# Stick attention: scores into the two x banks, logit sums on VectorE

## The chip, the cores and the metric

The kernel runs on one core of a Trainium2 chip. The metric is the device time of one execution in microseconds (us). Three timed executions of the kernel before gave 2578.15, 2578.38 and 2579.12 us, median 2578.38.

## The reference, cut to what matters

The program is two transformer blocks of two layers each, for 256 tokens of width 1024, in float32. The change lies in the mixer of the first layer of the first block, the stick-breaking attention with 16 heads of 64. For a query q and a key k before it (strictly causal):

```python
z = einsum(q, k) / 8
log_stay  = where(causal, log_sigmoid(-z), 0)
log_after = cumsum(log_stay, reverse=True) - log_stay
weights   = where(causal, exp(log_sigmoid(z) + log_after), 0)
out = weights @ v
```

log_sigmoid(-z) is -softplus(z), and softplus(z) = max(z, 0) + log(1 + exp(-|z|)). Taken together, the logarithm of a weight is z minus the sum of softplus over the keys from this one up to the query.

## The kernel before, in words

All stages run in one program; every engine executes its instructions in the order in which the Python code issues them (a manual schedule), and semaphores make one engine wait for another. `linear` (lines 364 to 366 are its matmuls) multiplies activations by weights that come from HBM, are split by ScalarE and VectorE into a high and a low part (lines 309 and 310) and are kept some tiles ahead. Its output blocks alternate between tiles of a pool of four PSUM banks (`self.ps()`, named p in the profile) and the two banks of `self.xp` (named xp), which are set aside for x in the last part of the program and lent to `linear` until then (`xp_lent`, lines 375 and 376). The odd blocks of a `linear` use xp, so the last block of the qkv product lies there until ScalarE has copied it out (line 775).

`stick` (from line 726) handles the 16 heads as eight pairs p. The scores are stored as keys by queries, 384 columns for each head of the pair. A pair goes through four stages:

- `stage_a(p)`: for each of the two heads e, four matmul instructions (lines 797 and 798) into a bank, then VectorE scales by 0.0625 (half of z) and adds the mask (line 799). Over both heads, 768 columns: VectorE forms min(-zh, zh) (line 800), ScalarE takes exp (line 801) and log(1+...) (line 803), and GpSimd forms zh - min (line 802).
- `stage_a2(p)`: GpSimd adds the two parts of softplus (line 808).
- `stage_b(p)`: TensorE sums softplus over keys with a triangular and an all-ones matrix (lines 817 to 819) into one bank for each head, VectorE forms 2·zh minus that (line 820), ScalarE takes exp (line 821).
- `stage_c(p)`: TensorE multiplies by v (lines 832 and 833) into one bank, and `put_split` writes the high part by ScalarE (line 543) and the low part by VectorE (line 544).

`round_(p)` (line 837) issues them as a pipeline: stage_a(p), stage_b(p-3), stage_a2(p), stage_c(p-5). Pairs 0 and 1 pass stage_a and stage_a2 earlier, beside the last block of the qkv product (deferred steps issued in `evac`). Rounds 2 to 7 thus have a new pair, rounds 3 to 10 a stage_b, rounds 5 to 12 a stage_c. Rounds up to 8 are issued before the output product `wo` begins, the last ones between its tiles. `wo` takes its first two banks from the same pool of four, after the bank that stage_c(2) used in round 7.

A round with all stages takes five banks of the pool of four: two in stage_a, two in stage_b, one in stage_c.

Of the kernel before, what the change touches and what calls it, by code (L numbers as in the profile page):

```python
# [9 lines left out]
AF = mybir.ActivationFunctionType  # L10
ALU = mybir.AluOpType
# [88 lines left out]
class Kernel:  # L100
# [625 lines left out]
    def stick(self):  # L726
        nc = self.nc
# [44 lines left out]
        def evac(n0, nw, ps):  # L772
            j, c = n0 // D, n0 % D
            for t in range(NT):
                nc.scalar.activation(qkv[j][t].ap[:, c:c + nw], ps[t], AF.Copy, scale=r()[:, t:t + 1])
            if c and j < 2:
                norm(j)
            if c and j == 1:
                self.defer(10, lambda: nc.scalar.preload_act_table_set("natural_log_exp_and_others"))
                self.defer(13, lambda: stage_a(0))  # L780
                self.defer(14, lambda: stage_a2(0))
                self.defer(15, lambda: stage_a(1))
                self.defer(16, lambda: stage_a2(1))

        mask = self.c[:, C_SBM:C_SBM + 384]
        tri, ones = self.c[:, C_TRI:C_TRI + 128], self.c[:, C_ONE:C_ONE + 128]
        st = {}

        def stage_a(p):


            q = qT[p // 4].ap[:, p % 4]
            zh, na, sp = (self.blk([128, 2, 384]) for _ in range(3))
            for e in range(2):
                k = kz[e][p // 4].ap[:, p % 4]
                z = self.ps()
                nc.tensor.matmul(z[:, :256], k[:, :128], q, start=True, stop=True)
                nc.tensor.matmul(z[:, 256:384], k[:, 128:], q[:, 128:], start=True, stop=True)
                nc.vector.scalar_tensor_tensor(zh.ap[:, e], z[:, :384], 0.0625, mask, op0=ALU.mult, op1=ALU.add)
            nc.vector.scalar_tensor_tensor(na.ap, zh.ap, -1.0, zh.ap, op0=ALU.mult, op1=ALU.min)  # L800
            nc.scalar.activation(sp.ap, na.ap, AF.Exp, scale=2.0)
            nc.gpsimd.tensor_tensor(na.ap, zh.ap, na.ap, ALU.subtract)
            nc.scalar.activation(sp.ap, sp.ap, AF.Ln, bias=1.0)
            st[p] = [zh, na, sp]

        def stage_a2(p):
            zh, m, sp = st[p]
            nc.gpsimd.tensor_tensor(sp.ap, m.ap, sp.ap, ALU.add)
            self.free(m)
            st[p] = [zh, sp]  # L810

        def stage_b(p):
            zh, sp = st[p]
            for e in range(2):
                inc = self.ps()
                s = sp.ap[:, e]
                nc.tensor.matmul(inc[:, :256], tri, s[:, :256], start=True, stop=False, skip_group_check=True)
                nc.tensor.matmul(inc[:, 128:256], ones, s[:, 256:], start=False, stop=True, skip_group_check=True)
                nc.tensor.matmul(inc[:, 256:384], tri, s[:, 256:], start=True, stop=True, skip_group_check=True)
                nc.vector.scalar_tensor_tensor(zh.ap[:, e], zh.ap[:, e], 2.0, inc[:, :384], op0=ALU.mult, op1=ALU.subtract)  # L820
            nc.scalar.activation(zh.ap, zh.ap, AF.Exp)
            self.free(sp)
            st[p] = zh

        def stage_c(p):
            w = st.pop(p)
# [10 lines left out]
        def round_(p):  # L837
            if 1 < p < 8:
                stage_a(p)
            if 0 <= p - 3 < 8:  # L840
                stage_b(p - 3)
            if 1 < p < 8:
                stage_a2(p)
            if 0 <= p - 5 < 8:
                stage_c(p - 5)
# [1258 lines left out]
```

## Time and profile before

| | |
|---|---|
| timed executions | 2578.15, 2578.38, 2579.12 us |
| profiled execution, its time | 2578.93 us |
| its span on the core | 2577.0 us |
| TensorE busy | 2332.2 us (91%) |
| VectorE busy | 1617.3 us (63%) |
| ScalarE busy | 897.1 us (35%) |
| GpSimd busy | 1058.4 us (41%) |
| mean granted TensorE clock | 0.97 of full speed |

The profiled execution took 2578.93 us, of which the span from the first to the last instruction is 2577.0 us. In the views, PE is TensorE's matmuls, PEld its weight loads, DVE VectorE, ACT ScalarE, POOL GpSimd, SP SyncE. L799 is line 799. A busy share over the whole span is a mean over stages with different limits; the stage that the change touches is a stretch of some 30 us around 280 us from the span's start.

### The profile page before, as it was taken

Reading aid. Unit: us, or ns where it says so; the run is one execution under the profiler, and the core shown is the slowest. Engines: PE = TensorE matmul, PEld = TensorE weight load, DVE = VectorE, ACT = ScalarE, POOL = GpSimd, SP = SyncE. Lnnn points to the kernel's source line nnn. Section 1 sums busy time; section 2 is a strip of 40 time slices with the busy share of each in tenths; the row PEclk is TensorE's granted clock in tenths of the full one; section 3 lists DMA queues with packets and bytes.
Section 4 is the critical chain, followed back from the end, with each engine's and each line's share of the span. In section 5 each row is a group of like instructions: output and inputs, shape, how many; then the busy total and the mean of one; then the engine's idle time right before and its main releaser. Section 6 shows DMA issues by size and latency. Waiting matters only on the chain.

```text
span 2577.0 us, 27968 instructions
## 1 busy us (share of the span) xinstructions
PE 2332.2 (91%) x8921; PEld 1516.9 (59%) x8921; DVE 1617.3 (63%) x3351; ACT 897.1 (35%) x1582; POOL 1058.4 (41%) x1119
## 2 busy tenths in 40 slices
PE   8999899999999999869998779997889898987877
PEld 7888688888888888755543234554344445432322
DVE  5555655555556556695687665854776764786744
ACT  5445554464445446521222211321222321222221
POOL 1002500000001001157677764655664665777775
PEclk9999999999999999989999989999999999999989
DMA  7555256565545654589999999999999999999998
GB/s 236 186 189 172 69 180 188 178 201 191 187 155 184 194 188 143 186 299 419 415 419 412 419 405 415 417 412 411 396 418 415 418 415 412 415 397 419 412 413 328
DMA packets 300786, 794.23 MB, mean 308 GB/s; under 512 B 26763, under 2 KB 66416, under 8 KB 300640
## 3 DMA queue, kind: packets, MB, share of 16 engines
q0 software_dynamic: 149152, 541.66, 52.1%
q1 hardware_dynamic: 151488, 250.78, 29.5%
q8 instruction: 72, 1.18, 0.2%
q14 instruction: 74, 0.61, 0.1%
HBM read 791.29 MB, written 1.05 MB: 307 GB/s over the span
## 4 chain that ended last, share of the span: by engine, by line
PE 61%; DMA 18%; DVE 12%; issue 4%; ACT 3%; POOL 1%; DVEq 0%; SPq 0%; POOLq 0%; ACTq 0%
PE p L1866 15%; DMA b<-in_peer_w_up,s 8%; PE p L364 6%; PE p L366 6%; PE p L365 6%; PE xp L364 6%; PE xp L366 6%; PE xp L365 6%; DMA b<-in_peer_w_down,s 6%; DVE b L1844 5%; PE p L1384 4%; DMA wr<-in_peer_w_q 3%; DMA wr<-in_dsa_w_in 1%; POOL b L1832 1%; PE p L1934 1%
## 5 line engine op out<-in xcount | busy, mean ns | idle before, releaser
L1866 PE MATMUL p<-b,s 128*128 128x512 f32 x2024 | 974.6, 621 | 147.1 <-ACT s L1864 93.9
L1866 PEld LDWEIGHTS p<-b,s 128*128 128x128 f32 x2024 | 380.6, 197 | 633.2 <-issue 490.9
L1844 DVE SCALAR_TENSOR_TENSOR b<-b,xp 128x1024 f32<-128x1024 f32 x512 | 610.2, 1212 | 141.9 <-DMA b<-in_peer_w_down,s 131.4
L1832 POOL DMA_INDIRECT b<-in_peer_w_down,s x512 | 482.8, 943 | 271.2 <-issue 95.4
L1832 POOL DMA_INDIRECT b<-in_peer_w_up,s x512 | 482.6, 942 | 259.4 <-issue 90.1
L310 DVE TENSOR_TENSOR wl<-wr,wh 128x1024 fp32r<-128x1024 f32 (+2 forms) x358 | 420.6, 1208 | 216.3 <-ACT wh L309 215.5
L309 ACT ACTIVATE wh<-wr 128x1024 fp32r<-128x1024 f32 (+2 forms) x358 | 361.6, 1040 | 199.6 <-PE xp L366 135.3
L653 POOL TENSOR_SCALAR s<-s 128x2 f32<-128x2 f32 (+1 forms) x12 | 4.8, 399 | 757.4 <-ACT b L662 727.3
L364 PE MATMUL p<-wh,b 128*128 128x512 f32 (+2 forms) x732 | 283.4, 387 | 1.5 <-DVE b L544 1.4
L366 PE MATMUL p<-wh,b 128*128 128x512 f32 (+2 forms) x732 | 277.1, 379 | 0.6 <-DVE b L544 0.3
L1864 ACT ACTIVATE s<-consts,s 128x128 f32<-128x128 f32 x506 | 175.3, 393 | 292.5 <-PE p L1866 169.8
L365 PE MATMUL p<-wl,b 128*128 128x512 f32 (+2 forms) x732 | 276.0, 377 | 0.1
L364 PE MATMUL xp<-wh,b 128*128 128x512 f32 (+3 forms) x716 | 273.1, 381 | 0.0
L366 PE MATMUL xp<-wh,b 128*128 128x512 f32 (+3 forms) x716 | 270.1, 377 | 0.0
L365 PE MATMUL xp<-wl,b 128*128 128x512 f32 (+3 forms) x716 | 269.9, 377 | 0.0
L366 PEld LDWEIGHTS p<-wh,b 128*128 128x128 f32 x732 | 137.9, 188 | 28.9 <-DVE b L548 2.9
L364 PEld LDWEIGHTS p<-wh,b 128*128 128x128 f32 x732 | 138.2, 189 | 27.0 <-DVE b L544 2.0
L1384 PE MATMUL p<-wr,b 128*128 128x512 f32 (+1 forms) x320 | 141.0, 566 | 13.9 <-DMA wr<-in_dsa_w_in 13.8
L365 PEld LDWEIGHTS p<-wl,b 128*128 128x128 f32 x732 | 138.4, 189 | 22.9 <-DVE wl L310 0.6
L366 PEld LDWEIGHTS xp<-wh,b 128*128 128x128 f32 x716 | 134.6, 188 | 24.6
L365 PEld LDWEIGHTS xp<-wl,b 128*128 128x128 f32 x716 | 134.8, 188 | 23.4
L364 PEld LDWEIGHTS xp<-wh,b 128*128 128x128 f32 x716 | 134.7, 188 | 23.5
(279 smaller groups left out, 1967.1 us busy)
## 6 DMA issues: line engine op xcount, KB each, us to landing
wr<-in_w_ffn_gu SPq DMA_DIRECT2D x176, 512.0 KB, 4.5
wr<-in_w_ffn_down SPq DMA_DIRECT2D x88, 512.0 KB, 4.5
wr<-in_dsa_w_in SPq DMA_DIRECT2D x56, 512.0 KB, 14.0
wr<-in_peer_w_q SPq DMA_DIRECT2D x40, 512.0 KB, 17.2
wr<-in_w_qkv SPq DMA_DIRECT2D x24, 512.0 KB, 4.5
wr<-in_w_ple_gate SPq DMA_DIRECT2D x16, 512.0 KB, 4.4
b<-in_peer_w_down,s POOLq DMA_INDIRECT x512, 9.1
b<-in_peer_w_up,s POOLq DMA_INDIRECT x512, 9.2
```

Of the source, the lines that this page charges most:

```text
L309: nc.scalar.activation(h, r, AF.Copy)
L310: nc.vector.tensor_tensor(l, r, h.bitcast(F32), ALU.subtract)
L364: nc.tensor.matmul(p[:, :nw], ah, h[:, kk, :], start=(k == 0), stop=False)
L365: nc.tensor.matmul(p[:, :nw], ah, l[:, kk, :], start=False, stop=False)
L366: nc.tensor.matmul(p[:, :nw], al, h[:, kk, :], start=False, stop=(k == last))
L653: nc.gpsimd.tensor_scalar(m, ss, mul, eps, op0=ALU.mult, op1=ALU.add)
L1384: nc.tensor.matmul(p[:, :nw], lhs(k0 + kk), w[:, kk, :], start=(k0 + kk == 0), stop=(k0 + kk == last), skip_group_check=True)
L1832: nc.gpsimd.indirect_dma_start(out=b.ap, out_offset=None, in_=(wd, wu)[s], in_offset=bass.IndirectOffsetOnAxis(ap=eidx[u][:, k:k + 1], axi ...
L1844: nc.vector.scalar_tensor_tensor(b.ap, b.ap, 1.0, self.xp, op0=ALU.mult, op1=ALU.mult, accum_out=acs[u][:, k:k + 1])
L1864: nc.scalar.activation(dg, self.ident, AF.Copy, scale=col)
L1866: nc.tensor.matmul(yp[n], dg, b.ap[:, n * 512:(n + 1) * 512], start=(h == 0 and k == 0), stop=(h == PH - 1 and k == (TOPK - 2 if u == nu - ...
L1934: nc.tensor.matmul(p[:, c * 128:(c + 1) * 128], w[:, kk, c * 128:(c + 1) * 128], xT1.ap[:, k], start=(k == 0 and c == 0), stop=(k == KD - ...
```

## The change

Pairs 2 to 7 write their scores into the two banks of xp, one for each head, instead of two banks of the pool; pairs 0 and 1 still use the pool. VectorE now scales by 0.125, so that the tile holds z itself. The instruction of line 800 writes min(-z, z) into the tile that exp and log then overwrite in place, so a pair holds two blocks of SBUF where it held three. GpSimd's two sums (lines 802 and 808) are gone; in stage_a2 one VectorE instruction forms max(z, 0) + log(1 + exp(-|z|)). In stage_b the subtraction needs no factor 2 and is a `tensor_tensor`. The order of the stages in `round_` is as it was.

```diff
         def stage_a(p):
             q = qT[p // 4].ap[:, p % 4]
-            zh, na, sp = (self.blk([128, 2, 384]) for _ in range(3))
+            z, sp = (self.blk([128, 2, 384]) for _ in range(2))
             for e in range(2):
                 k = kz[e][p // 4].ap[:, p % 4]
-                z = self.ps()
-                nc.tensor.matmul(z[:, :256], k[:, :128], q, start=True, stop=True)
-                nc.tensor.matmul(z[:, 256:384], k[:, 128:], q[:, 128:], start=True, stop=True)
-                nc.vector.scalar_tensor_tensor(zh.ap[:, e], z[:, :384], 0.0625, mask, op0=ALU.mult, op1=ALU.add)
-            nc.vector.scalar_tensor_tensor(na.ap, zh.ap, -1.0, zh.ap, op0=ALU.mult, op1=ALU.min)
-            nc.scalar.activation(sp.ap, na.ap, AF.Exp, scale=2.0)
-            nc.gpsimd.tensor_tensor(na.ap, zh.ap, na.ap, ALU.subtract)
+                s = self.xp[:, e * 512:(e + 1) * 512] if p > 1 else self.ps()
+                nc.tensor.matmul(s[:, :256], k[:, :128], q, start=True, stop=True)
+                nc.tensor.matmul(s[:, 256:384], k[:, 128:], q[:, 128:], start=True, stop=True)
+                nc.vector.scalar_tensor_tensor(z.ap[:, e], s[:, :384], 0.125, mask, op0=ALU.mult, op1=ALU.add)
+            nc.vector.scalar_tensor_tensor(sp.ap, z.ap, -1.0, z.ap, op0=ALU.mult, op1=ALU.min)
+            nc.scalar.activation(sp.ap, sp.ap, AF.Exp)
             nc.scalar.activation(sp.ap, sp.ap, AF.Ln, bias=1.0)
-            st[p] = [zh, na, sp]
+            st[p] = [z, sp]
 
         def stage_a2(p):
-            zh, m, sp = st[p]
-            nc.gpsimd.tensor_tensor(sp.ap, m.ap, sp.ap, ALU.add)
-            self.free(m)
-            st[p] = [zh, sp]
+            z, sp = st[p]
+            nc.vector.scalar_tensor_tensor(sp.ap, z.ap, 0.0, sp.ap, op0=ALU.max, op1=ALU.add)
 
         def stage_b(p):
...
-                nc.vector.scalar_tensor_tensor(zh.ap[:, e], zh.ap[:, e], 2.0, inc[:, :384], op0=ALU.mult, op1=ALU.subtract)
-            nc.scalar.activation(zh.ap, zh.ap, AF.Exp)
+                nc.vector.tensor_tensor(z.ap[:, e], z.ap[:, e], inc[:, :384], ALU.subtract)
+            nc.scalar.activation(z.ap, z.ap, AF.Exp)
```

## Rows read from the trace of the kernel before

**Rows 1.** Busy time by stretch: PE, PEld, DVE, ACT, POOL, then PEclk, DMA share, GB/s.

```profile
280.00:308.00 28.00, 20.31 (x126) 16.33 (x127) 22.06 (x31) 14.71 (x21) 25.70 (x13) 1.00 0.00 1
322.00:400.00 78.00, 78.00 (x365) 64.55 (x361) 44.48 (x50) 41.82 (x53) 0.90 (x2) 1.00 0.56 176
```

**Rows 2.** Timeline of VectorE: start, length, then [idle before <- who ended it].

```profile
276.10 0.96 DVE L800 SCALAR_TENSOR_TENSOR b<-b 128x768 f32<-128x768 f32 x1
276.98 1.02 DVE L799 SCALAR_TENSOR_TENSOR b<-p,consts 128x384 f32<-128x384 f32 x2
278.03 2.62 DVE L800 SCALAR_TENSOR_TENSOR b<-b 128x768 f32<-128x768 f32 x1
...
283.07 1.00 DVE L820 SCALAR_TENSOR_TENSOR b<-b,p 128x384 f32<-128x384 f32 x2
288.39 1.01 DVE L799 SCALAR_TENSOR_TENSOR b<-p,consts 128x384 f32<-128x384 f32 x2
...
294.78 0.42 DVE L544 TENSOR_TENSOR b<-p,b 128x256 fp32r<-128x256 f32 x1 [1.92 <-ACT b L543]
295.13 1.01 DVE L799 SCALAR_TENSOR_TENSOR b<-p,consts 128x384 f32<-128x384 f32 x2
...
307.08 0.42 DVE L544 TENSOR_TENSOR b<-p,b 128x256 fp32r<-128x256 f32 x1 [1.92 <-ACT b L543]
```

**Rows 3.** Timeline of GpSimd, and busy time of L800 alone in the rounds.

```profile
278.02 1.82 POOL L802 TENSOR_TENSOR b<-b,b 128x768 f32<-128x768 f32 x1 [3.96 <-ACT b L801]
...
276.90:304.40 27.50, 13.13 (x7) 1.00 0.05 17
```

**Rows 4.** Timeline of ScalarE.

```profile
277.10 0.84 ACT L801 ACTIVATE b<-b 128x768 f32<-128x768 f32 x1 [3.49 <-DVE b L800]
277.97 0.84 ACT L803 ACTIVATE b<-b 128x768 f32<-128x768 f32 x1
278.84 1.26 ACT L775 ACTIVATE b<-xp,s 128x512 f32<-128x512 f32 x2
...
279.43 0.68 ACT L775 ACTIVATE b<-xp,s 128x512 f32<-128x512 f32 x1
...
292.91 0.84 ACT L803 ACTIVATE b<-b 128x768 f32<-128x768 f32 x1
293.66 0.83 ACT L821 ACTIVATE b<-b 128x768 f32<-128x768 f32 x1
294.39 0.36 ACT L543 ACTIVATE b<-p 128x256 fp32r<-128x256 f32 x1
```

**Rows 5.** Timeline of TensorE: end of the qkv product, two pairs' scores, start of wo.

```profile
272.35 0.39 PE L366 MATMUL xp<-wh,b 128*128 128x512 f32 x1
...
281.27 0.67 PE L797 MATMUL p<-b,b 128*128 128x256 f32 x2 [1.64 <-DVE b L799]
...
282.43 0.38 PE L798 MATMUL p<-b,b 128*128 128x128 f32 x2
...
307.56 0.50 PE L364 MATMUL p<-wh,b 128*128 128x512 f32 x1 [0.85 <-DVE b L544]
```

**Rows 6.** A later idle stretch: TensorE's timeline, and busy time with PEclk.

```profile
1138.57 1.97 PE L589 MATMUL q<-consts,b 128*128 128x128 f32 x8 [5.79 <-DVE b L1159]
1140.33 3.68 PE L504 MATMUL p<-b,b 128*128 128x256 f32 x8
1144.42 1.89 PE L504 MATMUL p<-b,b 128*128 128x256 f32 x8
...
1137.00:1138.00 1.00, 0.00 (x0) 0.00 (x0) 0.85 (x6) 0.00 (x0) 0.54 (x1) 0.66 1.03 417
1144.00:1145.00 1.00, 1.00 (x8) 0.95 (x7) 1.00 (x3) 0.00 (x0) 0.69 (x2) 0.92 0.86 332
...
1110.00:1120.00 10.00, 8.13 (x23) 5.84 (x24) 8.88 (x29) 2.04 (x6) 2.81 (x3) 0.50 0.87 313
```

More of the change, by code (lines that the diff above doesn't have):

```diff
@@ L792, in stage_a @@
             q = qT[p // 4].ap[:, p % 4]
-            zh, na, sp = (self.blk([128, 2, 384]) for _ in range(3))
+            z, sp = (self.blk([128, 2, 384]) for _ in range(2))
             for e in range(2):
                 k = kz[e][p // 4].ap[:, p % 4]
-                z = self.ps()
-                nc.tensor.matmul(z[:, :256], k[:, :128], q, start=True, stop=True)
-                nc.tensor.matmul(z[:, 256:384], k[:, 128:], q[:, 128:], start=True, stop=True)
-                nc.vector.scalar_tensor_tensor(zh.ap[:, e], z[:, :384], 0.0625, mask, op0=ALU.mult, op1=ALU.add)
-            nc.vector.scalar_tensor_tensor(na.ap, zh.ap, -1.0, zh.ap, op0=ALU.mult, op1=ALU.min)
-            nc.scalar.activation(sp.ap, na.ap, AF.Exp, scale=2.0)
-            nc.gpsimd.tensor_tensor(na.ap, zh.ap, na.ap, ALU.subtract)
+                s = self.xp[:, e * 512:(e + 1) * 512] if p > 1 else self.ps()
[4 more added lines that the diff above has]
+            nc.scalar.activation(sp.ap, sp.ap, AF.Exp)
             nc.scalar.activation(sp.ap, sp.ap, AF.Ln, bias=1.0)
-            st[p] = [zh, na, sp]
+            st[p] = [z, sp]
         def stage_a2(p):
-            zh, m, sp = st[p]
-            nc.gpsimd.tensor_tensor(sp.ap, m.ap, sp.ap, ALU.add)
-            self.free(m)
-            st[p] = [zh, sp]
+            z, sp = st[p]
+            nc.vector.scalar_tensor_tensor(sp.ap, z.ap, 0.0, sp.ap, op0=ALU.max, op1=ALU.add)
         def stage_b(p):
-            zh, sp = st[p]
+            z, sp = st[p]
             for e in range(2):
@@ L819, in stage_b @@
                 nc.tensor.matmul(inc[:, 256:384], tri, s[:, 256:], start=True, stop=True, skip_group_check=True)
-                nc.vector.scalar_tensor_tensor(zh.ap[:, e], zh.ap[:, e], 2.0, inc[:, :384], op0=ALU.mult, op1=ALU.subtract)
-            nc.scalar.activation(zh.ap, zh.ap, AF.Exp)
+                nc.vector.tensor_tensor(z.ap[:, e], z.ap[:, e], inc[:, :384], ALU.subtract)
+            nc.scalar.activation(z.ap, z.ap, AF.Exp)
             self.free(sp)
-            st[p] = zh
+            st[p] = z
         def stage_c(p):
```

## The prediction

> **What bounds the kernel now.** I first read the busy time by stretch, to see what limits the place that is touched. In 280 to 308 us, where the rounds of the stick attention run, no engine is full: VectorE is busy for 22.06 of 28 us, GpSimd for 25.70, TensorE for 20.31, DMA does nothing; from 322 us on TensorE is busy for 78.00 of 78 us [rows 1]. So what the rounds lose or gain reaches the end undiminished: behind them stands an engine that is always busy, and the weights for it have long arrived. One bound for all of this: the stretch is about 30 of 2577 us, and 0.2% of the time, about what a measurement of this kernel can tell from no change, is 5.2 us.
>
> Then I read the timelines of VectorE, ScalarE, GpSimd and TensorE there. VectorE sets the pace in the order of the code: the two score instructions L799, then L800, then stage_b's two L820, then L544, and the next L799. Two things lengthen it. L800 takes 0.96 us alone, but 2.62 us at 278.03, where GpSimd's L802 began 0.01 us earlier and ran 1.82 us [rows 2, 3]; over the rounds it is busy 13.13 us, of which 0.16 us belong to the end of pair 1's [rows 3]. And where a round has a stage_c, VectorE stands idle for 1.92 us before L544, which needs ScalarE's L801, L803, L821 and L543 one behind the other [rows 2, 4]. The three rounds without stage_c take from 276.98 to 288.39, 11.41 us in all; the three with it run from there to the L544 at 307.08, whose end lets `wo` begin at 307.56 [rows 2, 5].
>
> **The change, part by part.**
>
> *GpSimd's sums go.* Nothing then lengthens L800: six times 0.96 instead of 13.13 - 0.16 = 12.97 us, 7.2 us less busy time [rows 2, 3]. The Trainium skill has this in "SBUF — State Buffer", section "Who interferes with whom": a VectorE instruction with two SBUF inputs and a GpSimd one that reads SBUF exclude each other, and the later one waits until the other has finished. By that rule alone the sum would be a gain; it is the fourth case below. GpSimd's queue holds only the loads of p for the next ffn behind the sums; they start earlier and stay hidden.
>
> *One VectorE sum comes, behind a wait.* It has the shape and operands of L800, so 0.96 us, and the next instruction starts 0.88 us after it (276.10 to 276.98 [rows 2]). Its tile comes from the log, L803, so VectorE's whole queue stands behind ScalarE in every round. From L799 on: L800 1.05 later (276.98 to 278.03 [rows 2]); L801 1.00 after that (276.10 to 277.10 [rows 2, 4]); L803 0.87 later (277.10 to 277.97); its end passed on another 0.87 later, as to the next on ScalarE at 278.84 [rows 4]. The new sum so starts at 1.05 + 1.00 + 0.87 + 0.87 = 3.79 and the next L799 at 4.67. The two subtractions of stage_b (1.00 us for both, from PSUM, like L820; dropping the factor 2 saves nothing, since L544, also a `tensor_tensor` from PSUM, takes 0.42 us for 256 columns and L820 pays about 0.5 for 384 [rows 2]) lie between L800 and the sum, in 1.93 to 2.93, inside the wait. Only their cover is new; uncovered they would cost 1.0 a round.
>
> *Rounds with a stage_c.* ScalarE goes on from L803 to L821 in 0.75 and L543 in 0.73 (292.91, 293.66, 294.39 [rows 4]), L544 follows in 0.39 and the next L799 in 0.35 (294.78, 295.13 [rows 2]). L544 starts at 1.05 + 1.00 + 0.87 + 0.75 + 0.73 + 0.39 = 4.79, behind the end of the sum (4.67), and the round takes 5.14. The sum costs nothing here: ScalarE's chain covers it.
>
> *The banks.* Three pool banks a round instead of five: TensorE need not wait for the pool and can run a round ahead, so VectorE never waits for it at full clock. I cost that at nothing beyond what the round lengths hold. `wo` still takes the bank that stage_c(2) leaves, so it still starts behind that L544.
>
> *Pair 2 waits for x's banks.* Before, pair 2's scores were done during the end of the qkv product, so its L799 came at 276.98 [rows 2]. Now they go into the banks that hold qkv's last block until L775 has copied them out. The first copy starts at 278.84 and takes 0.68, to 279.52 [rows 4]; TensorE starts 0.06 later as at 307.50 to 307.56 [rows 2, 5], at 279.58. A pair's scores take from 281.27 to 282.81, 1.54 us [rows 5], to 281.12; half of L799's 1.02 and two hand-overs of 0.03 follow, and L800 of pair 2 starts at 281.72. That corresponds to an L799 of both heads at 280.67, 3.7 us later than before. Pair 1's new sum waits for the log that ends at 278.81 [rows 4], is out of the way at 279.7, and is hidden by this; pair 0's lies in idle time of VectorE.
>
> *The clock.* TensorE ends the qkv product at 272.74 [rows 5] and now has nothing until 279.58: 6.8 us. After an idle stretch of 5.79 us the granted clock was 0.66 in the last stretch shown before work came, so it had gone to 1.2 GHz, and it was 0.92 at 1144 to 1145, 5.5 us after TensorE had begun to work back to back at 1138.57 [rows 6]. I take the same here. Eight matmuls of 256 columns took 3.68 us at half clock and 1.89 mostly at full, 0.224 more each [rows 6]; a pair's scores are six such lengths (four of 256, four of 128 columns), so pair 2 starts 1.34 us later still. Bounds: nothing, if the clock holds, and the third case below, if it stays low. The pairs behind cost nothing more: TensorE has scores 2, scores 3 and sums 0 queued (6 + 6 + 8 lengths at 0.46, 9.2 us without a pause), and VectorE needs those later than that. The Trainium skill speaks against the change here: "TensorE: Matmul & The Clock Gate", section "Why this matters for your kernels", asks for no idle gaps between bursts of matmuls, since they bring the half rate. Without that rule and that row the sum would be 1.34 smaller.
>
> **The sum.** Start 280.67 + 1.34 = 282.01. Rounds 2 to 4: 3 × 4.67 = 14.01 (11.41 before). Rounds 5 and 6: 2 × 5.14 = 10.28. Round 7 to L544: 4.79, and 0.48 to `wo` (307.08 to 307.56 [rows 2, 5]): 5.27. Together 29.56: `wo` starts at 311.57 instead of 307.56, **4.0 us later**. Everything behind has the same order and lengths. The profiled execution took 2578.93 us, 0.55 above the median of the runs and within their spread; 2578.93 + 4.0 would be its own time after, and against the median it is 2578.4 + 4.0 = **2582.4 us**. The six rounds between start and `wo` gain 30.58 - 29.56 = 1.0 us; the late start (3.7) and the clock (1.34) take 5.0.
>
> **The rivals.**
> 1. *The forecast*: x's banks come free late, the clock falls and returns. 0.60.
> 2. *The clock holds.* Only the idle stretch speaks for it falling; where in it the fall comes can differ. 2578.4 + 2.7 = 2581.1 us. 0.10.
> 3. *The clock stays low* (slower than before by more than can be missed). In 1110 to 1120 us it stayed at 0.50 for ten us with TensorE busy 81% [rows 6], so pauses can keep it down. A round's scores and sums are 14 lengths, 6.4 us at 0.46, and stage_c's up to 2.8 us more; take 7.8, against a round of 5.14: TensorE becomes the bound, 2.7 us a round. It decides once the low clock lasts into round 5, some 296 us. One round gives 2585.1, three 2590.5. Against it: the 9.2 us without a pause, longer than the 5.5 us that brought the clock back. 0.15.
> 4. *The freed port decides alone*: the wait for the log and the banks cost nothing, and VectorE's balance is 7.2 us less in L800 and 6 × 0.88 = 5.3 us more in the new sum: 2576.5 us. Against it: the order in the code puts the sum ahead of the next scores. 0.08.
> 5. *VectorE runs without any wait* from 276.98: scores and L800 1.05 + 0.88, new sum 0.88, stage_b's two 0.93, L544 0.35 (0.48 to `wo`), so rounds of 2.81, 3.74, 3.74, 4.09, 4.09 and 4.22, 22.7 us, `wo` 7.9 us earlier: 2570.5 us. This is the floor, and needs ScalarE's chain to be hidden, which the 1.92 us of rows 2 deny. 0.04.
>
> 0.03 is left for what none of these names, on both sides.
>
> **How the numbers follow.** 0.2% lies at 2573.2 and 2583.5 us. Slower: case 3 (0.15) and the upper sixth of case 1, since hand-overs of 0.03 to 0.06 a step over six rounds can add the 1.1 us that are missing (0.10): 0.25. Faster: case 5 and half of the rest, 0.05. Same: 0.70. The range 2577.5 to 2586.0 takes cases 1 and 2 with their bounds and the shorter half of case 3; case 5, most of case 4 and the longer half of case 3 stay outside.
>
> **What would show it.** VectorE's first L799 of pair 2 at about 281 and L800 of pair 2 at 283 (281.7 if the clock holds); granted clock 0.5 between about 278 and 285; all L800 at 0.96; VectorE idle some 0.8 us before each new sum, which ScalarE's log ends; rounds of 4.7 and then 5.1 us; `wo` at 311.6. Wrong would be the step on the banks if pair 2's scores start before L775 ends, the step on the sum if VectorE does not wait for the log, and the clock's if rounds 5 to 7 are longer than 5.3 us with TensorE as the one waited for.

## The result, and the profile after

The changed kernel takes 2593.92 us (median of five runs, 2591.47 to 2595.66); the kernel before takes 2578.96 us beside it (2578.15 to 2579.47). The ratio is 1.0058, with a 95% interval of 1.0046 to 1.0069: slower by 15 us, where 4 were forecast and the range ended at 2586.0. The direction had been given a chance of 0.25.

Two of the first lines of the profile's page, of the changed kernel:

```profile
span 2592.1 us, 27928 instructions
PE 2341.9 (90%) x8921; PEld 1524.6 (59%) x8921; DVE 1620.2 (63%) x3359; ACT 897.9 (35%) x1582; POOL 1028.0 (40%) x1103
```

Over the span hardly anything moves: GpSimd loses 30 us of busy time (1058.4 before), VectorE gains 3, TensorE 10. Such lines can't say where 15 us went. The span grew by 2592.1 - 2577.0 = 15.1 us, so the next thing to read is the stretch that was touched, by its two ends in TensorE's timeline: the last matmul of the qkv product and the first of `wo`. In the changed kernel:

```profile
273.19 0.40 PE L366 MATMUL xp<-wh,b 128*128 128x512 f32 x1
280.72 1.22 PE L796 MATMUL xp<-b,b 128*128 128x256 f32 x2 [7.13 <-ACT b L775]
283.09 1.22 PE L796 MATMUL xp<-b,b 128*128 128x256 f32 x2 [0.72 <-DVE b L798]
285.38 1.22 PE L796 MATMUL xp<-b,b 128*128 128x256 f32 x2 [0.65 <-DVE b L798]
...
302.46 1.22 PE L796 MATMUL xp<-b,b 128*128 128x256 f32 x2 [2.44 <-DVE b L798]
...
315.76 0.88 PE L796 MATMUL xp<-b,b 128*128 128x256 f32 x2 [1.91 <-DVE b L798]
...
323.60 0.50 PE L364 MATMUL p<-wh,b 128*128 128x512 f32 x1
```

From 273.19 to 323.60 are 50.41 us; before, 272.35 to 307.56 [rows 5], 35.21 us. The difference of 15.20 us is the whole loss. This distance is the yardstick of all that follows, and it is called **the stretch** from here on.

The rows also show how it was lost. The first pair that uses x's banks (pair 2) starts behind L775, as forecast. But then its second head's scores (283.09) wait for VectorE's L798, and that is the read of the *first* head's scores, in the other bank: the VectorE timeline of the same kernel has it at 282.47, ending at 283.03.

```profile
279.40 0.96 DVE L806 SCALAR_TENSOR_TENSOR b<-b,b 128x768 f32<-128x768 f32 x1 [1.78 <-ACT b L801]
282.47 0.56 DVE L798 SCALAR_TENSOR_TENSOR b<-xp,consts 128x384 f32<-128x384 f32 x1 [2.11 <-PE xp L797]
284.77 0.56 DVE L798 SCALAR_TENSOR_TENSOR b<-xp,consts 128x384 f32<-128x384 f32 x1 [1.74 <-PE xp L797]
285.36 0.96 DVE L799 SCALAR_TENSOR_TENSOR b<-b 128x768 f32<-128x768 f32 x1
288.11 0.96 DVE L806 SCALAR_TENSOR_TENSOR b<-b,b 128x768 f32<-128x768 f32 x1 [1.78 <-ACT b L801]
288.98 0.55 DVE L798 SCALAR_TENSOR_TENSOR b<-xp,consts 128x384 f32<-128x384 f32 x1
...
296.02 0.55 DVE L798 SCALAR_TENSOR_TENSOR b<-xp,consts 128x384 f32<-128x384 f32 x1
297.65 0.56 DVE L798 SCALAR_TENSOR_TENSOR b<-xp,consts 128x384 f32<-128x384 f32 x1 [1.07 <-PE xp L797]
...
301.86 0.55 DVE L798 SCALAR_TENSOR_TENSOR b<-xp,consts 128x384 f32<-128x384 f32 x1
...
308.92 0.55 DVE L798 SCALAR_TENSOR_TENSOR b<-xp,consts 128x384 f32<-128x384 f32 x1
...
315.16 0.55 DVE L798 SCALAR_TENSOR_TENSOR b<-xp,consts 128x384 f32<-128x384 f32 x1
```

(The lines have moved: L796 and L797 are the scores that were L797 and L798, L798 is the scaling that was L799, L799 the minimum that was L800, L806 the new sum.) Before, the two scalings were one row, x2, 1.02 us long [rows 2]. Now TensorE and VectorE take turns: scores of head 0, read, scores of head 1, read. At 285.38 the next pair's scores wait in the same way for the read of head 1, though their bank was read two us before (282.47 to 283.03). The view of who waited for whom, from 270 to 326 us, has these rows among others:

```profile
DVE b L798 <- PE xp L797: 10.8, 7, 2.1
...
PE xp L796 <- DVE b L798: 10.2, 7, 2.6
...
PE xp L796 <- ACT b L775: 7.1, 1, 7.1
...
DVE b L806 <- ACT b L801: 7.1, 5, 1.8
```

Columns are us in total, times, longest. Of the last row, one wait of 1.8 us belongs to pair 0's sum, ahead of the stretch. Waits of the last two kinds were in the forecast; the first two, each the other's cause, were not. And TensorE's clock, by stretch (after the busy times: granted clock, DMA share, GB/s):

```profile
278.00:295.00 17.00, 10.36 (x30) 8.31 (x31) 6.85 (x10) 5.98 (x8) 0.00 (x0) 0.52 0.05 18
302.00:306.00 4.00, 3.54 (x12) 3.13 (x13) 2.08 (x4) 0.27 (x1) 0.00 (x0) 0.57 0.00 0
316.00:320.00 4.00, 4.00 (x16) 3.44 (x15) 2.07 (x3) 1.28 (x2) 0.00 (x0) 0.57 0.00 0
```

It fell in the gap, as forecast, but stayed at 1.2 GHz for 17 us instead of 7, and fell twice more. Rounds 2 to 4, from one head-0 L798 to the next, took 6.51, 7.04 and 5.84 us (288.98 - 282.47, 296.02 - 288.98, 301.86 - 296.02), where 4.67 was forecast; rounds 5 and 6 took 7.06 and 6.24 us (308.92 - 301.86, 315.16 - 308.92), where 5.14 was.

### The profile page after: what moved, and what is told of

Read it like the earlier page. It is cut to its first block, busy times and chain, and to the rows that moved or that the text cites. A ratio compares the mean times of both kernels' runs of the same rounds, so it can differ in the third digit from the quotient of the medians.

```text
span 2592.1 us, 27928 instructions
## 1 busy us (share of the span) xinstructions
PE 2341.9 (90%) x8921; PEld 1524.6 (59%) x8921; DVE 1620.2 (63%) x3359; ACT 897.9 (35%) x1582; POOL 1028.0 (40%) x1103
## 4 chain that ended last, share of the span: by engine, by line
PE 61%; DMA 18%; DVE 11%; issue 5%; ACT 3%; POOL 2%; SPq 0%; DVEq 0%; POOLq 0%; ACTq 0%
PE p L1862 14%; DMA b<-in_peer_w_up,s 7%; DMA b<-in_peer_w_down,s 7%; PE p L364 6%; PE p L366 6%; PE xp L364 6%; PE xp L366 6%; PE xp L365 6%; PE p L365 6%; DVE b L1840 4%; PE p L1380 4%; DMA wr<-in_peer_w_q 2%; POOL b L1828 2%; DMA wr<-in_dsa_w_in 1%; PE p L504 1%
## 5 line engine op out<-in xcount | busy, mean ns | idle before, releaser
L310 DVE TENSOR_TENSOR wl<-wr,wh 128x1024 fp32r<-128x1024 f32 (+2 forms) x358 | 420.5, 1208 | 213.6 <-ACT wh L309 212.7
```

Of the source, the lines that this page charges most:

```text
L310: nc.vector.tensor_tensor(l, r, h.bitcast(F32), ALU.subtract)
```

## The experiments

Theory T: x's two banks are one tile (one buffer that the program allocates as a whole) for the program's synchronization, so a write into either waits for the last read of either. Rivals: C, the low clock after the gap is the main cost; W, the wait of VectorE's new sum for the log is; L, the late start of pair 2 is.

The experiments ran on two other chips, on which the part of the program from about 1000 us on takes longer: the kernel before takes 2721.54 and 2725.84 us there (medians), and nearly all runs of one kernel lie within 18 to 27 us. That spread is larger than most of the differences asked for, so the stretch, from one profile of each kernel, is the measurement to go by; ratios are given beside it. Up to `wo` the chips agree: the last matmul of the qkv product starts at 271.9 to 273.2 us in every run, and pair 1's first scaling 2.42 to 2.44 us behind it in all seven kernels with VectorE's sums, 2.70 or 2.71 in the three with GpSimd's. No kernel was profiled twice, so a few hundredths in the table mean nothing.

| kernel | stretch, us | against before |
|---|---|---|
| before | 35.21 | |
| changed | 50.41 | +15.20 |
| scores first | 40.13 | +4.92 |
| own tiles | 36.68 | +1.47 |
| banks only | 46.15 | +10.94 |
| sums only | 36.65 | +1.44 |
| pair 2 in the pool | 45.57 | +10.36 |
| clock held | 46.29 | +11.08 |
| reordered | 27.74 | -7.47 |
| order on before | 32.49 | -2.72 |

**Scores first.** One loop becomes two: the same instructions on each engine, in the same order there; only the reads now stand behind both writes in the program.

```diff
             for e in range(2):
...
                 nc.tensor.matmul(s[:, 256:384], k[:, 128:], q[:, 128:], start=True, stop=True)
-                nc.vector.scalar_tensor_tensor(z.ap[:, e], s[:, :384], 0.125, mask, ...)
+                sc.append(s)
+            for e in range(2):
+                nc.vector.scalar_tensor_tensor(z.ap[:, e], sc[e][:, :384], 0.125, mask, ...)
```

> The changed kernel, but the scores of both heads are issued before VectorE reads either. Theory T (the two banks are ordered as one tile: a write into either waits for the last read of either, so head 1's scores wait for head 0's L798 and TensorE can't run ahead): the waits of TensorE on L798 between the two heads (0.7 to 1.1 us in six pairs) and the VectorE waits on L797 that follow (1.1 to 1.7 us) go, rounds come down to 4.7 and 5.1 us, wo starts some 11 us earlier than at 323.6, about 2583 us. Theory C (the low clock after the gap is what costs, the order hardly matters): the clock still falls in the same gap, about 2590 us or more. Theory W (VectorE's wait for the log costs more than the 0.8 us a round seen): no change, 2593.

Measured: 40.13 us, 10.28 less than the changed kernel; ratio to before 1.0017 (0.9995 to 1.0039). TensorE and VectorE timelines of this run:

```profile
280.16 1.22 PE L797 MATMUL xp<-b,b 128*128 128x256 f32 x2 [7.13 <-ACT b L775]
...
284.27 1.22 PE L797 MATMUL xp<-b,b 128*128 128x256 f32 x2 [1.19 <-DVE b L801]
```

```profile
283.19 1.02 DVE L801 SCALAR_TENSOR_TENSOR b<-xp,consts 128x384 f32<-128x384 f32 x2 [3.39 <-PE xp L798]
284.25 0.96 DVE L802 SCALAR_TENSOR_TENSOR b<-b 128x768 f32<-128x768 f32 x1
...
287.87 1.02 DVE L801 SCALAR_TENSOR_TENSOR b<-xp,consts 128x384 f32<-128x384 f32 x2
...
292.54 1.01 DVE L801 SCALAR_TENSOR_TENSOR b<-xp,consts 128x384 f32<-128x384 f32 x2
...
297.21 1.01 DVE L801 SCALAR_TENSOR_TENSOR b<-xp,consts 128x384 f32<-128x384 f32 x2
...
302.35 1.01 DVE L801 SCALAR_TENSOR_TENSOR b<-xp,consts 128x384 f32<-128x384 f32 x2
...
307.49 1.01 DVE L801 SCALAR_TENSOR_TENSOR b<-xp,consts 128x384 f32<-128x384 f32 x2
```

The scalings are a pair again (x2), and the rounds are 4.68, 4.67, 4.67, 5.14 and 5.14 us: the forecast's 4.67 and 5.14 within a hundredth. From the first of them to `wo` are 312.76 - 283.19 = 29.57 us, where the prediction had 29.56. The gap is still there, and so is the low clock; full clock was back by 288 us:

```profile
287.00:288.00 1.00, 1.00 (x4) 0.82 (x4) 1.00 (x2) 0.00 (x0) 0.00 (x0) 0.53 0.00 0
288.00:289.00 1.00, 1.00 (x10) 0.95 (x9) 0.97 (x3) 0.00 (x0) 0.00 (x0) 1.00 0.00 0
```

Theory T has its main number, and theories C and W fall as the main cost: the clock's first fall and the wait for the log are both still in this run. The pair's reads still wait for both heads' scores (3.39 before 283.19), and the next pair's scores at 284.27 for both reads; so the one tile still costs something at the start, though nothing in the rounds.

**Own tiles.** The scores go to the transposes' banks, a pool of two tiles (named q).

```diff
-                s = self.xp[:, e * 512:(e + 1) * 512] if p > 1 else self.ps()
+                s = self.pst() if p > 1 else self.ps()
```

> The changed kernel, but pairs 2 to 7 put their scores into the two banks of the transposes' pool, two tiles of their own, instead of the two banks of x's tile. Theory T: head 1 no longer waits for head 0's read, and pair 2 need not wait for the qkv product to be copied out; VectorE then begins pair 2 when pair 1's new sum is done (some 279.7 us in the clock of the trace before), wo starts 1.7 us later than before: about 2580.6 us. Theory C: the gap of TensorE moves behind pair 2's scores and is still over 5 us, the clock still falls, so most of the loss stays: about 2588. Theory W: 2593.

Measured: 36.68 us, ratio 1.0001 (0.9977 to 1.0025). A row of TensorE and one of VectorE:

```profile
272.26 0.59 PE L796 MATMUL q<-b,b 128*128 128x256 f32 x2
```

```profile
279.13 1.02 DVE L798 SCALAR_TENSOR_TENSOR b<-q,consts 128x384 f32<-128x384 f32 x2
```

With two tiles of their own, pair 2's scores run right behind the qkv product, the scalings are again one row for both heads, and neither the turns nor the wait for the qkv product are left. The clock fell here too, in the gap behind pair 2's scores (0.52 from 276 to 283 us), and it cost nothing: VectorE waited for TensorE in no round. What remains, 1.47 us, is the price of the sums on VectorE in this order.

**Banks only** and **sums only** are the two halves of the change: the kernel before with x's banks for pairs 2 to 7 and GpSimd's sums kept, and the changed kernel with all scores in the pool of four.

```diff
-                z = self.ps()
+                z = self.xp[:, e * 512:(e + 1) * 512] if p > 1 else self.ps()
```

> The kernel before with the banks of x for the scores of pairs 2 to 7 and nothing else: GpSimd keeps its two sums. Theory T: nearly the whole loss is here: late start 3.7 and 1 to 2 us of low clock, 1.1 us more in each of six rounds, TensorE unable to run ahead: 2588 to 2594 us. If the two banks were independent: 2583 to 2584. Theory W (the new sum costs): near 2579 to 2583.

> The changed kernel with the scores in the pool of four as before: only GpSimd's sums go to VectorE. Theory T: this part costs little: rounds of 4.7 (no stage_c) and 5.1 to 5.5 us, start of pair 2 at 279.7 in the clock of the trace before, about 2580 to 2582 us, TensorE waiting a little for the pool. Theory W: the wait for the log is what costs, 2588 or more. Freed port alone: 2576.5.

Measured: banks only 46.15 us, 10.94 more than before, ratio 1.0048 (1.0021 to 1.0075); sums only 36.65 us, 1.44 more, ratio 1.0014 (0.999 to 1.0038). In the terms of the first chip that is 2578.4 + 10.9 = 2589.3 us, inside the 2588 to 2594 of theory T, and 2578.4 + 1.4 = 2579.8, just below its 2580 to 2582. The two halves make 12.4 of the 15.2 us; the other 2.8 come only with both together. With banks only, the clock stayed at 1.00 from 292 us on, while in the changed kernel it fell twice more; what those two falls cost was not measured by itself. The VectorE timeline of banks only has both troubles in one round, the turns and GpSimd:

```profile
298.12 0.54 DVE L799 SCALAR_TENSOR_TENSOR b<-xp,consts 128x384 f32<-128x384 f32 x1
299.68 0.56 DVE L799 SCALAR_TENSOR_TENSOR b<-xp,consts 128x384 f32<-128x384 f32 x1 [1.01 <-PE xp L798]
300.27 2.47 DVE L800 SCALAR_TENSOR_TENSOR b<-b 128x768 f32<-128x768 f32 x1
```

The sums-only run equals the run with own tiles within 0.03 us, so three pool banks a round instead of five, which the change was to gain, were worth nothing here.

**Pair 2 in the pool.** `p > 1` becomes `p > 2`.

> The changed kernel with pair 2 also in the pool of four; x's banks only from pair 3 on. Measured from the last qkv matmul to the first of wo (before 35.2 us, changed kernel 50.4, scores first 40.1, own tiles 36.7). Theory T: pair 2 starts some 3.7 us earlier, the order inside x's tile stays for five pairs: about 46 us, of which the five pairs' waits are 5 to 6 us and the low clock the rest. Theory L (the late start of pair 2 is most of the loss, by way of the gap and the clock): below 40 us.

Measured: 45.57 us, from a single run. Theory L falls: pair 2's scaling starts 7.10 us behind the last qkv matmul, as with own tiles, and the loss is still 10.36 of 15.20. The gap has moved behind pair 2's scores and the clock still fell in it (0.50 from 276 to 288 us), so the 10.36 us hold its price too.

**Clock held.** Ahead of pair 2's scores, seven matmuls whose result nobody reads.

```diff
+            if p == 2:
+                f = self.pst()
+                for _ in range(7):
+                    nc.tensor.matmul(f, self.ident, self.c[:, :512], start=True, stop=True)
```

> The changed kernel with seven matmuls of 512 columns whose result nobody reads, in the gap ahead of pair 2's scores, so that TensorE does not stand idle there. Theory T: the granted clock stays at 1.0 into pair 2; pair 2's scores take 0.7 us less a head and the first rounds 5.8 us instead of 6.5 and 7.0; the waits of head 1's scores on head 0's L798 stay. 46 to 48 us from the last qkv matmul to wo (50.4 without). Theory C (the clock is the main cost): 41 us or less, near the 40.1 of the run with the scores first.

Measured: 46.29 us, from a single run. TensorE's timeline, and the clock by stretch:

```profile
273.45 6.17 PE L796 MATMUL q<-consts 128*128 128x512 f32 x14
280.75 0.70 PE L800 MATMUL xp<-b,b 128*128 128x256 f32 x2 [1.13 <-ACT b L775]
...
282.39 0.70 PE L800 MATMUL xp<-b,b 128*128 128x256 f32 x2 [0.72 <-DVE b L802]
...
288.16 1.22 PE L800 MATMUL xp<-b,b 128*128 128x256 f32 x2 [3.28 <-DVE b L802]
```

```profile
278.00:288.00 10.00, 4.38 (x16) 2.41 (x14) 4.35 (x6) 4.33 (x6) 0.00 (x0) 1.00 0.07 28
288.00:292.00 4.00, 3.84 (x14) 3.43 (x15) 2.07 (x4) 0.56 (x1) 0.00 (x0) 0.57 0.00 0
```

With full clock in pair 2 the scores take 0.70 instead of 1.22 a row, and head 1 still waits 0.72 us for head 0's read. So the turns do not come from the clock. Without its first fall the stretch is 4.12 us shorter (50.41 - 46.29). That need not be the whole price of the low clock: a pause of 3.28 us, which ends at 288.16, stands before another fall, and the second round took 6.50 us where 5.8 was expected.

**Reordered.** If the forecast's round lengths are right, what limits the rounds without the turns is VectorE's wait for the log and for ScalarE's chain to L544. Both can be had out of the way by order alone: stage_c behind the scores and the minimum, exp and log after it, and the new sum one pair later.

```diff
-                s = self.xp[:, e * 512:(e + 1) * 512] if p > 1 else self.ps()
+                s = self.pst() if p > 1 else self.ps()
...
         def round_(p):
             if 1 < p < 8:
                 stage_a(p)
+            if 0 <= p - 5 < 8:
+                stage_c(p - 5)
+            if 1 < p < 8:
+                stage_a1(p)
             if 0 <= p - 3 < 8:
                 stage_b(p - 3)
-            if 1 < p < 8:
-                stage_a2(p)
-            if 0 <= p - 5 < 8:
-                stage_c(p - 5)
+            if 1 < p < 9:
+                stage_a2(p - 1)
```

(stage_a1 is exp and log, taken out of stage_a; pair 1's sum moves from the qkv product into round 2.)

> Two tiles of their own for the scores (the transposes' banks), sums on VectorE, and a new order in the round: scores and L799, then stage_c, then exp and log, then stage_b, then the new sum of the pair before. If the wait for the log and the stage_c chain on ScalarE are what limits the rounds once the bank order is gone (as the prediction's round lengths say), rounds come to 2.8, 3.7 and 4.1 us, wo starts about 27.5 us after the last qkv matmul (35.2 before), and the time is 6 to 8 us below the kernel before. If TensorE or the clock limits: 32 to 35 us, no gain.

Measured: 27.74 us, 7.47 less than before; 2716.13 us against 2725.84, ratio 0.997 (0.995 to 0.9989). Two rounds in VectorE's timeline, first and last row of each shown, and the first row of the next:

```profile
288.17 1.02 DVE L797 SCALAR_TENSOR_TENSOR b<-q,consts 128x384 f32<-128x384 f32 x2
...
291.36 0.95 DVE L810 SCALAR_TENSOR_TENSOR b<-b,b 128x768 f32<-128x768 f32 x1
292.23 1.01 DVE L797 SCALAR_TENSOR_TENSOR b<-q,consts 128x384 f32<-128x384 f32 x2
...
295.41 0.95 DVE L810 SCALAR_TENSOR_TENSOR b<-b,b 128x768 f32<-128x768 f32 x1
296.28 1.01 DVE L797 SCALAR_TENSOR_TENSOR b<-q,consts 128x384 f32<-128x384 f32 x2
```

These two full rounds take 4.06 and 4.05 us, without a wait on any row: the prediction's floor of 4.09. Of the expected 2.8, 3.7 and 4.1 us one round missed: pair 3's took 4.19, with the granted clock at 0.57 from 278 to 282 us. By the stretch this version beats both kernels, and the interval of the ratio to before lies below 1.

**Order on before.** The same order in the kernel before, with GpSimd's sums and the pool of four.

> The kernel before with only the new order of the round: GpSimd keeps its sums, scores in the pool of four. If the order alone pays: about 29 to 31 us from the last qkv matmul to wo, 4 to 6 us below the kernel before, short of the reordered kernel by the time L800 loses to GpSimd. If VectorE's freed port is needed for it: 33 to 35 us, hardly a gain.

Measured: 32.49 us, 2.72 less than before; ratio 0.9973 (0.9952 to 0.9994). The stretch lies between the two expectations, nearer to the second; the ratio's interval holds it (2.72 of 2725 us less is 0.999). The ratios of this run and the reordered one can't tell the two apart; by the stretch, about a third of the reordered kernel's gain is the order alone. In VectorE's timeline the minimum still loses to GpSimd, 0.96 us of work taking 2.31:

```profile
291.30 2.31 DVE L799 SCALAR_TENSOR_TENSOR b<-b 128x768 f32<-128x768 f32 x1
```

So moving the sums to VectorE pays 32.49 - 27.74 = 4.75 us in this order, in which VectorE does not wait for the log, and cost 1.44 in the old one. (The two kernels compared differ in the scores' banks as well; in the old order that made no difference, in the new one it was not tried.)

## Why the prediction was wrong

**The step that failed** is "The banks": "TensorE need not wait for the pool and can run a round ahead, so VectorE never waits for it at full clock. I cost that at nothing". The forecast took the two halves of x's tile for two independent buffers. They are one tile, and the program orders a write into either half behind the last read of either. That made TensorE and VectorE take turns and cost 50.41 - 40.13 = 10.28 us, two thirds of the loss. At full clock the turns lengthened a round by 1.17 us (5.84 for 4.67, round 4) or 1.10 (6.24 for 5.14, round 6); for six rounds that is an estimated 6.8 us, and the rest of the 10.28 would be the low clock that the turns prolong. The same assumption stands in the step on the clock: scores 2, scores 3 and sums 0 were to follow each other "without a pause", but scores 3 had to wait for the reads of scores 2. The trace of before could have raised the question but not shown the answer: `linear` writes both halves and then reads both, so there the order of the two never mattered. That the wait goes when the reads are issued after both writes, and when the same scores go into two separate tiles, shows that it is the program's ordering by tile and not a property of the banks. How that ordering is made up inside stays open.

The signs that the prediction set did not point at this step. Pair 2's scores did not start before L775 ended, so the sign for the banks stayed away; rounds 5 to 7 were longer than 5.3 us (7.06, 6.24 and, to its L544, 6.72) with VectorE waiting for TensorE, which was the sign for the clock, but round 6 took 6.24 us at full clock (1.00 from 308 to 315 us).

**The late start** was right in kind and too small. By the runs, the wait for x's banks with the low clock behind it is 40.13 - 36.68 = 3.45 us. The prediction's own terms for the same two, against a start behind pair 1's new sum (278.84 + 0.88 = 279.72 in the clock of before), are 280.67 - 279.72 = 0.95 and 1.34, together 2.3. The other 1.2 us are again the one tile: the scores waited for the second copy of L775 instead of the first, in the changed kernel as with the scores first, some 0.6 us (1.27 for both copies, 0.68 for one [rows 4]), and the reads for both heads' scores, which puts both scalings behind them, an estimated half of 1.02 us more. (The prediction's 281.72 also holds a slip of 0.03: 281.12 + 0.51 + 0.06 is 281.69.)

```profile
279.40 1.27 ACT L775 ACTIVATE b<-xp,s 128x512 f32<-128x512 f32 x2
```

**The clock** fell as forecast, and with the scores first its price was about the forecast's 1.34 us: pair 2's scores took from 280.16 to 283.08, 2.92 us where 1.54 are needed at full clock [rows 5], and full clock was back by 288 us. In the changed kernel the turns put pauses into TensorE's work, the clock stayed low to 295.7 us, and the first fall cost 4.12 us. A clock that stays low was the third rival's start, given 0.15, but the rival had TensorE's own work as what then bounds the rounds, and not the turns. The Trainium skill's rule in "TensorE: Matmul & The Clock Gate", section "Why this matters for your kernels", against idle gaps between bursts of matmuls, agrees with the first fall, behind 7.13 us without work. The two later falls lie behind shorter pauses, behind which the clock held in other runs (last section).

**The sum on VectorE** was right within a hundredth: rounds of 4.67 and 5.14 us with the scores first, a wait of 0.86 us for the log in each, 1.79 where no stage_b covers it. Its whole cost was forecast, without the banks, at 279.72 + 29.56 - 307.56 = 1.72 us and measured at 1.44 and 1.47. The difference is a gain that the prediction overlooked: without GpSimd's sums, VectorE's L310 ahead of pair 1 takes 1.23 us instead of 1.50, and pair 1 starts 0.28 us earlier.

**GpSimd's sums** were right too: every minimum takes 0.96 us in the changed kernel. The Trainium skill's rule in "SBUF — State Buffer", section "Who interferes with whom", that a VectorE instruction with two SBUF inputs and a GpSimd one that reads SBUF exclude each other, agrees with that, and with the 2.47 us with banks only, where GpSimd kept its sums.

**The fifth rival**, VectorE without waits, did not come true in this order but was a correct floor: 7.9 us below before was its price, and the reordered kernel reached 7.47.

## What to carry to other kernels

In this program a PSUM tile of two banks was one buffer where synchronization is concerned: before lending halves of such a tile to a pipeline, give each half its own tile, or issue all writes of a step ahead of all its reads. When an operation moves to the engine that sets the pace, its operands' lateness moves with it; place it behind work that does not need them, here one pair later, and the move pays.

## What the runs showed of the hardware that was not expected

The length of a pause did not tell whether the clock would fall behind it. In the changed kernel a pause of 1.91 us (ended at 315.76) stood before a fall in 316 to 320 us (0.57 in the windows above), and one of 2.44 us (ended at 302.46) before another. With pair 2 in the pool, a pause of 2.44 us that ended at 297.16 brought no fall (1.00 from 296 to 300 us), and of two pauses of 1.91 us the first brought none (1.00 from 302 to 306 us) and the second one did (0.56 from 310 to 311 us):

```profile
303.40 0.70 PE L796 MATMUL xp<-b,b 128*128 128x256 f32 x2 [1.91 <-DVE b L798]
...
309.64 0.80 PE L796 MATMUL xp<-b,b 128*128 128x256 f32 x2 [1.91 <-DVE b L798]
```

What made the difference stays open. With the scores first, a pause of 1.19 us at 284.27 did not keep the clock from coming back, and it held at 1.0 from 288 to 300 us. From the first scores behind the gap to full clock it took 15 us in the changed kernel (280.72 to 295.7) and less than 8 with the scores first (280.16 to 288).
